# Output projection of a retention/S5/cross-attention block: model columns instead of tokens on the partitions

## Chip, cores and metric

The kernel runs on one core of a Trainium2 chip. The metric is the device time of one execution in microseconds (us); each kernel is run several times and the median is compared.

## What is computed

The reference is one block of a sequence model over 1024 tokens of 1024 features: retention and an S5 branch with an output projection and a residual, then cross-attention to a memory of 256 rows, and a final norm. The part that matters here is its end:

```python
    o = jnp.einsum('bhlm,bmhd->blhd', p, va).reshape(B, L, XA_HEADS * XA_DH)
    x = x + o @ xa_wo[l]
return rms_norm(x, norm_f_g)     # y = x * rsqrt(mean(x*x, -1) + EPS);  y * g
```

## The kernel before, in words

All activations are held transposed (features on the 128 partitions, tokens in the free dimension), each as a pair of float32r tiles, a high part and a low part. A matrix product is three matmuls per 128-deep slice of the contraction: high by high, high by low and low by high (`mm3`, lines 94 to 97). Weights come in groups of 256 columns: `get_w` (line 84) hands out the group that is ready and starts the load of the next one, which `load_w` (line 65) brings in two DMAs on the SyncE queue (line 70) and splits into its high part on ScalarE (line 74) and its low part on VectorE or GpSimd (line 75). The planner of the framework writes the order of each engine's instructions ahead of the run; the program's order is only its starting point, so work of neighbouring stages is interleaved.

The last stages (lines 902 to 1002) handle two halves of 512 tokens. `scores` and `attend` make the attention output `oT` of a half, feature-major. `wo_half` (line 944) then multiplies it by the output weights, for four groups `gi` of 256 model columns. The second half's `attend` calls are put between the groups of the first half (`between`, line 955); `wo_half` of the second half has nothing between.

In one group, `wo_half` goes over the four 128-token blocks in pairs. For each pair:

- the residual `x1`, which lies feature-major, is read from DRAM in two DMAs per group (line 953), turned by four TensorE transposes into the PSUM tile `pxps` (line 962), and copied to the tile `on` by ScalarE (line 963);
- per token block 24 matmuls (8 slices by 3) go into the PSUM tile `wops`, with 128 tokens as the stationary operand and the 256 weight columns moving (line 968);
- VectorE adds the residual (line 972), ScalarE squares with an accumulated row sum (line 974), and for the first three groups VectorE multiplies by the norm's gain (line 976).

At the fourth group `finish` (line 983) adds up the row sums (one column per token block), takes a reciprocal square root by bit trick and three Newton steps (`rsqrt`, lines 111 to 120: eleven small VectorE instructions), scales one half of the row on ScalarE (line 989) and the other on VectorE (lines 991 and 992), and sends the two pieces of 128 rows by 512 columns to the output (lines 990 and 993, SyncE queue). The PSUM pool for `wops` has two buffers of two banks.

Two helpers are used elsewhere in the program and matter here: `mean_sq` (line 271) sums squares over the partitions by matmuls against a column of ones, one matmul of one moving column per 128 tokens, and `bcast_rows` (line 122) spreads a per-token scalar over all partitions by a matmul of the scalar (broadcast to 128x128) with the identity.

Of the kernel before, what the change touches and what calls it, by code (L numbers as in the profile page):

```python
# [12 lines left out]
F32 = mybir.dt.float32  # L13
F32R = mybir.dt.float32r
I32 = mybir.dt.int32
AF = mybir.ActivationFunctionType
ALU = mybir.AluOpType
AX = mybir.AxisListType
PSUM = bass.MemoryType.PSUM

P = 128
L = 1024
D = 1024
# [7 lines left out]
EPS = 1e-6  # L31
# [14 lines left out]
def block_kernel(ctx: ExitStack, tc: tile.TileContext, a: dict):  # L46
    nc = tc.nc
    v, s, g = nc.vector, nc.scalar, nc.gpsimd
# [6 lines left out]
    small = ctx.enter_context(tc.tile_pool(name="small", bufs=2, reuse_waits="tile"))  # L55
# [6 lines left out]
    def sm_ps(shape, name="smps"):  # L62
        return psm.tile(shape, F32, tag="sm", name=name)
# [30 lines left out]
    def mm3(out, wh, wl, xh, xl, first, last):  # L94
        nc.tensor.matmul(out, wh, xh, start=first, stop=False)  # L95
        nc.tensor.matmul(out, wh, xl, start=False, stop=False)  # L96
        nc.tensor.matmul(out, wl, xh, start=False, stop=last)  # L97
# [13 lines left out]
    def rsqrt(dst, x, m, name):  # L111

        it = small.tile([P, m], I32, tag="rsq_i", name=f"i_{name}")
        t = small.tile([P, m], F32, tag="rsq_t", name=f"t_{name}")
        v.tensor_scalar(it, x.bitcast(I32), 1, None, op0=ALU.logical_shift_right)
        v.tensor_scalar(dst.bitcast(I32), it, -1.0, RSQ, op0=ALU.mult, op1=ALU.add)
        for _ in range(3):
            v.tensor_tensor(t, dst, dst, ALU.mult)
            v.scalar_tensor_tensor(t, t, -0.5, x, op0=ALU.mult, op1=ALU.mult)
            v.scalar_tensor_tensor(dst, t, 1.5, dst, op0=ALU.add, op1=ALU.mult)  # L120
# [14 lines left out]
    off = {}  # L135
# [3 lines left out]
        o += width  # L139
    ident, cmask, gv, geps, g128, gn_g = (off[z] for z in ("ident", "cmask", "gv", "geps", "g128", "gn_g"))  # L140
    g2, gm, glu_b, invf, rsgn, nsgn, psgn = (off[z] for z in ("g2", "gm", "glu_b", "invf", "rsgn", "nsgn", "psgn"))
    d4, i16 = off["d4"], off["i16"]
    g1 = gp1
    ones = const.tile([P, 1], F32, name="ones")
    v.memset(ones, 1.0)
# [53 lines left out]
    for k in range(KT):  # L199
# [5 lines left out]
        hi, lo = act_pair(k, "h")  # L205
        s.activation(w_hi[:, k, :], wr, AF.Copy)
        for c in ((slice(0, 512), slice(512, L)) if k == 0 else (slice(0, L),)):
# [3 lines left out]
                                   op0=ALU.mult, op1=ALU.subtract)  # L211
# [472 lines left out]
    for gi in range(4):  # L684
        w = get_w("w_u", gi)
        for c in range(2):
            ct = 2 * gi + c
            ps = proj_t(w, c, hT, name="ups")
            ut = ev.tile([P, 8, 8, 16], F32, tag="ut", name=f"ut{ct}", bufs=3)
            pv = ps.rearrange("p q (n j c) -> p (q n) j c", n=4, j=8)  # L690
            rb = rstd_b.rearrange("p (n j c) -> p n j c", n=8, j=8)
# [158 lines left out]
    kalo = ap_.tile([P, 8, M], F32R, name="kalo")  # L850
    vahi = ap_.tile([P, 2, D], F32R, name="vahi")
    valo = ap_.tile([P, 2, D], F32R, name="valo")
    gf = ap_.tile([P, D], F32, name="gf")
    nc.sync.dma_start(out=gf, in_=a["gf"].to_broadcast([P, D]))
    qap = ctx.enter_context(tc.tile_pool(name="qap", bufs=2, reuse_waits="tile"))

    def queries(half, h):
# [84 lines left out]
            lst.append((hi, lo))  # L942

    def wo_half(half, oT, between):
        on = [qap.tile([P, D], F32, tag=("qhi", "qlo")[t % 2], name=f"on{half}{t}") for t in range(4)]
        ssq = [small.tile([P, 5], F32, tag=f"ssq{t}", name=f"ssq{half}{t}") for t in range(4)]
        pre = [z[:, 4:5] for z in ssq]
        for gi in range(4):
            hi, lo = get_w("w_xo", gi)
            xts = []  # L950
            for c in range(2):
                xt = pp.tile([P, 512], F32, tag="xt", name=f"xt{half}{gi}{c}", bufs=4)
                nc.sync.dma_start(out=xt, in_=a["x1_d"][2 * gi + c][:, half * 512:half * 512 + 512])
                xts.append(xt)
            between(gi)
            cs = slice(gi * 256, gi * 256 + 256)
            for t0 in range(0, 4, 2):
                px = sm_ps([P, 2, 256], "pxps")
                for t in range(2):
                    ts = slice((t0 + t) * P, (t0 + t + 1) * P)  # L960
                    for c in range(2):
                        nc.tensor.transpose(px[:, t, c * P:c * P + P], xts[c][:, ts], ident)
                    s.activation(on[t0 + t][:, cs], px[:, t, :], AF.Copy)
                ps = big_ps([P, 2, 512], "wops")
                for t in range(2):
                    ts = slice((t0 + t) * P, (t0 + t + 1) * P)
                    for k in range(8):
                        mm3(ps[:, t, 0:256], oT[k][0][:, ts], oT[k][1][:, ts], hi[:, k, :], lo[:, k, :],
                            k == 0, k == 7)
                for t in range(2):  # L970
                    x2 = on[t0 + t]
                    v.tensor_tensor(x2[:, cs], ps[:, t, 0:256], x2[:, cs], ALU.add)
                    jk = pp.tile([P, 256], F32, tag="jk", name="jk", bufs=2)
                    s.activation(jk, x2[:, cs], AF.Square, accum_out=ssq[t0 + t][:, gi:gi + 1])
                    if gi < 3:
                        v.tensor_tensor(x2[:, cs], x2[:, cs], gf[:, cs], ALU.mult)
                    if gi == 2:
                        v.tensor_reduce(pre[t0 + t], ssq[t0 + t][:, 0:3], axis=AX.X, op=ALU.add)
                        v.tensor_scalar(pre[t0 + t], pre[t0 + t], 1.0 / D, EPS, op0=ALU.mult, op1=ALU.add)
                    if gi == 3:  # L980
                        finish(half, t0 + t, x2, ssq[t0 + t][:, 3:4], pre[t0 + t])

    def finish(half, t, x2, last, pre):
        ss = small.tile([P, 1], F32, tag="ssf", name="ssf")
        rf = small.tile([P, 1], F32, tag="rf", name="rf")
        v.scalar_tensor_tensor(ss, last, 1.0 / D, pre, op0=ALU.mult, op1=ALU.add)
        rsqrt(rf, ss, 1, "f")
        row = (half * 4 + t) * P
        s.activation(x2[:, 0:512], x2[:, 0:512], AF.Copy, scale=rf)
        nc.sync.dma_start(out=a["out"][row:row + P, 0:512], in_=x2[:, 0:512])  # L990
        v.scalar_tensor_tensor(x2[:, 768:D], x2[:, 768:D], rf, gf[:, 768:D], op0=ALU.mult, op1=ALU.mult)
        v.tensor_scalar(x2[:, 512:768], x2[:, 512:768], rf, None, op0=ALU.mult)
        nc.sync.dma_start(out=a["out"][row:row + P, 512:D], in_=x2[:, 512:D])

    pr0, pr1, oT0, oT1 = [], [], [], []
    for h in range(4):
# [1 line left out]
    for h in range(4):  # L998
# [13 lines left out]


CPACK = (("ident", 128), ("cmask", 128), ("gv", 8), ("geps", 8), ("g128", 4), ("gn_g", 8), ("g2", 8), ("gm", 8),
         ("glu_b", 8), ("invf", 1), ("rsgn", 1), ("nsgn", 1), ("psgn", 1), ("d4", 16), ("i16", 16))
CPW = sum(z for _, z in CPACK)


def tok_perm():
    return np.arange(L).reshape(NCH, 16, 8).transpose(0, 2, 1).reshape(L)  # L1020


def host_arrays(x, mem, positions, norm1_g, w_in, ret_gn_g, s5_a_re, s5_a_im, s5_log_dt,
# [4 lines left out]
    def c(z):  # L1028
        return np.ascontiguousarray(z)

    def col(vec):
        return c(np.asarray(vec).reshape(8, P).T)
# [14 lines left out]
    out = {}  # L1047
# [2 lines left out]
    out["g1"], out["g2"] = col(np.asarray(norm1_g)[0]), col(np.asarray(norm2_g)[0])  # L1050
    out["gm"] = col(np.asarray(norm_mem_g)[0])
    out["gn_g"] = col(np.asarray(ret_gn_g)[0])
    out["gf"] = c(np.asarray(norm_f_g).reshape(1, D))
    out["glu_b"] = col(np.asarray(s5_glu_b)[0][chp])
    out["w_kq"], out["w_v"], out["w_g"] = wg(w_kq), wg(wv), wg(wgr)
    out["w_u"], out["w_gs"] = wg(wu[:, chp]), wg(wgs[:, chp])
# [60 lines left out]
```

## Time and profile before

| | us |
|---|---|
| median of 3 runs | 1185.98 (1185.93 to 1187.71) |
| the profiled execution's own time | 1183.76 |
| span of its profile | 1182.0 |
| TensorE busy in the span | 1132.4 (96%) |
| VectorE / ScalarE / GpSimd busy | 640.4 / 451.0 / 284.6 |
| mean granted TensorE clock | 0.979 |

The span runs from the first to the last instruction of the profiled execution; 1.76 us of its own time lie outside. Below, PE is TensorE, PEld its weight load, DVE VectorE, ACT ScalarE, POOL GpSimd, SPq the SyncE queue that issues DMAs. In a row of a timeline the first number is the start in us from the beginning of the span, the second the duration in us; "x2" means that neighbouring instructions were merged. Ends of matmuls are modelled, so the steps from start to start tell more than the durations.

### The profile page before, as it was taken

What the parts mean: (1) busy time and instruction counts of PE and PEld (TensorE: products, weight loads), DVE (VectorE), ACT (ScalarE), POOL (GpSimd) and SP (SyncE); (2) the same over time, 40 slices, a digit from 0 to 9 for tenths busy, and PEclk for the clock granted to TensorE, in tenths of its full rate; (3) what the DMA queues carried; (4) which work ended last, traced back from release to release, by engine and by line L of the source; (5) the groups of instructions that cost most, each with busy time, mean ns of one, the idle gap of its engine ahead of it and who ended that gap; (6) DMA issues with size and microseconds to landing.
All of it is one profiled execution on the core that took longest, in us unless ns stands there. A gap on an engine that the chain in (4) does not pass through costs nothing.

```text
span 1182.0 us, 18361 instructions
## 1 busy us (share of the span) xinstructions
PE 1132.4 (96%) x7020; PEld 991.8 (84%) x7020; DVE 640.4 (54%) x1348; ACT 451.0 (38%) x903; POOL 284.6 (24%) x422
## 2 busy tenths in 40 slices
PE   8899689999999689999999999999999999999996
PEld 6897688898888568888888888888889888889996
DVE  7794464573662425585577216534635445554564
ACT  7322432342432312354453115224334444444453
POOL 2348798372084101212221100000320000000000
PEclk9899899999999889999999999999999999999998
DMA  6412343343241177799785349534446522222251
GB/s 233 120 52 89 98 159 131 101 153 97 55 165 58 36 225 202 212 279 276 222 268 202 133 148 279 179 124 148 137 143 197 173 77 72 72 72 72 90 197 72
DMA packets 92376, 171.88 MB, mean 145 GB/s; under 512 B 10880, under 2 KB 46976, under 8 KB 92288
## 3 DMA queue, kind: packets, MB, share of 16 engines
q1 hardware_dynamic: 92000, 170.57, 45.7%
q8 instruction: 55, 0.90, 0.3%
q14 instruction: 33, 0.27, 0.1%
q10 hardware_dynamic: 288, 0.14, 0.0%
HBM read 122.04 MB, written 44.43 MB: 141 GB/s over the span
## 4 chain that ended last, share of the span: by engine, by line
PE 59%; DMA 2%; DVE 2%; ACT 1%; issue 0%; DVEq 0%; ACTq 0%
PE wops L95 3%; PE wops L96 3%; PE wops L97 3%; PE qaps L97 3%; PE qaps L96 3%; PE gsps L97 2%; PE glups L95 2%; PE glups L97 2%; PE qaps L95 2%; PE gsps L96 2%; PE gsps L95 2%; PE obps L96 2%; PE obps L95 2%; PE obps L97 2%; PE glups L96 2%; PE oaps L97 2%
## 5 line engine op out<-in xcount | busy, mean ns | idle before, releaser
L95 PE MATMUL vps<-whi_w_v,hh 128*128 128x256 f32 x256 | 73.5, 287 | 0.7 <-ACT qs_k L290 0.7
L96 PE MATMUL vps<-wlo_w_v,hh 128*128 128x256 f32 x256 | 73.5, 287 | 0.6 <-POOL wlo_w_v L75 0.6
L95 PE MATMUL wops<-whi_w_xo,o 128*128 128x256 f32 x256 | 73.6, 288 | 0.0
L97 PE MATMUL vps<-whi_w_v,hl 128*128 128x256 f32 x256 | 73.5, 287 | 0.0
L97 PE MATMUL wops<-whi_w_xo,o 128*128 128x256 f32 x256 | 72.1, 281 | 0.0
L95 PE MATMUL gps<-whi_w_g,hh 128*128 128x256 f32 x256 | 71.9, 281 | 0.0
L96 PE MATMUL wops<-wlo_w_xo,o 128*128 128x256 f32 x256 | 71.8, 281 | 0.0
L97 PE MATMUL gps<-whi_w_g,hl 128*128 128x256 f32 x256 | 71.8, 281 | 0.0
L96 PE MATMUL gps<-wlo_w_g,hh 128*128 128x256 f32 x256 | 71.5, 279 | 0.0
L844 POOL TENSOR_TENSOR sq<-sq,sqx 128x1024 f32<-128x1024 f32 x7 | 19.0, 2717 | 196.9 <-ACT sqx L843 196.9
L95 PE MATMUL ups<-hh,whi_w_u 128*128 128x512 f32 x128 | 51.9, 406 | 1.9 <-DVE ut L692 1.9
L95 PEld LDWEIGHTS vps<-whi_w_v,hh 128*128 128x128 f32 x256 | 49.8, 194 | 1.8 <-ACT qs_k L290 1.1
L96 PE MATMUL ups<-hl,whi_w_u 128*128 128x512 f32 x128 | 51.2, 400 | 0.0
L97 PE MATMUL ups<-hh,wlo_w_u 128*128 128x512 f32 x128 | 51.2, 400 | 0.0
L96 PEld LDWEIGHTS vps<-wlo_w_v,hh 128*128 128x128 f32 x256 | 49.8, 195 | 1.6 <-POOL wlo_w_v L75 0.8
L95 PE MATMUL oaps<-reth,whi_w_oa 128*128 128x512 f32 x128 | 51.0, 398 | 0.0
L97 PE MATMUL qaps<-h,wlo_w_xq 128*128 128x512 f32 x128 | 50.6, 396 | 0.0
L95 PE MATMUL gsps<-hh,whi_w_gs 128*128 128x512 f32 x128 | 50.6, 395 | 0.0
L97 PE MATMUL gsps<-hh,wlo_w_gs 128*128 128x512 f32 x128 | 50.6, 395 | 0.0
L95 PE MATMUL qaps<-h,whi_w_xq 128*128 128x512 f32 x128 | 50.5, 394 | 0.0
L96 PE MATMUL qaps<-h,whi_w_xq 128*128 128x512 f32 x128 | 50.4, 394 | 0.0
L97 PE MATMUL oaps<-reth,wlo_w_oa 128*128 128x512 f32 x128 | 50.3, 393 | 0.0
(394 smaller groups left out, 3496.2 us busy)
## 6 DMA issues: line engine op xcount, KB each, us to landing
CS<-tab_d SPq DMA_DIRECT2D x32, 256.0 KB, 5.2
yr<-y_d SPq DMA_DIRECT2D x16, 512.0 KB, 6.2
wraw_w_xq<-w_xq SPq DMA_DIRECT2D x16, 512.0 KB, 4.1
wraw_w_xo<-w_xo SPq DMA_DIRECT2D x16, 512.0 KB, 4.4
vv_d<-VV SPq DMA_DIRECT2D x16, 288.0 KB, 2.8
VV<-vv_d SPq DMA_DIRECT2D x16, 288.0 KB, 4.3
wraw_w_v<-w_v SPq DMA_DIRECT2D x8, 512.0 KB, 4.6
wraw_w_g<-w_g SPq DMA_DIRECT2D x8, 512.0 KB, 4.8
```

Of the source, the lines that this page charges most:

```text
L95: nc.tensor.matmul(out, wh, xh, start=first, stop=False)
L96: nc.tensor.matmul(out, wh, xl, start=False, stop=False)
L97: nc.tensor.matmul(out, wl, xh, start=False, stop=last)
L844: g.tensor_tensor(sq2, sq2, sq, ALU.add)
```

## The change

The projection is turned over: the weight columns become the stationary operand (128 model columns) and 512 tokens move, so the result comes out feature-major, as the residual lies in DRAM. The transposes of the residual and their ScalarE copies are gone; VectorE adds the residual straight from the loaded tile. Squares are summed in a tile `acc` over the eight column blocks (the additions on GpSimd, in the last group on VectorE), and `finish` then sums `acc` over the partitions by `mean_sq`, takes the reciprocal square root for up to four token blocks in one chain, spreads it over the partitions by matmuls into PSUM (`rb`), and scales eight column blocks on VectorE, each with its gain as a per-partition scalar, each followed by its own output DMA. In the last group of the second half the 512 tokens are handled in two parts of 256. The output tensor is laid out (8, 128, 1024) and is turned back on the host. The gain comes in the packed constants instead of a 512 KB broadcast load.

```diff
-    gf = ap_.tile([P, D], F32, name="gf")
-    nc.sync.dma_start(out=gf, in_=a["gf"].to_broadcast([P, D]))
...
     def wo_half(half, oT, between):
-        on = [qap.tile([P, D], F32, tag=("qhi", "qlo")[t % 2], name=f"on{half}{t}") for t in range(4)]
-        ssq = [small.tile([P, 5], F32, tag=f"ssq{t}", name=f"ssq{half}{t}") for t in range(4)]
-        pre = [z[:, 4:5] for z in ssq]
+        x2 = [qap.tile([P, 2, 512], F32, tag=("qhi", "qlo")[t % 2], name=f"x2_{half}{t}") for t in range(4)]
+        acc = pp.tile([P, 512], F32, tag="acc", name=f"acc{half}", bufs=2)
         for gi in range(4):
...
             between(gi)
...
+            parts = [slice(0, 512)] if gi < 3 or half == 0 else [slice(0, 256), slice(256, 512)]
+            for ts in parts:
                 ps = big_ps([P, 2, 512], "wops")
+                for c in range(2):
+                    cs = slice(c * P, c * P + P)
                     for k in range(8):
-                        mm3(ps[:, t, 0:256], oT[k][0][:, ts], oT[k][1][:, ts], hi[:, k, :], lo[:, k, :],
-                            k == 0, k == 7)
...
+                        mm3(ps[:, c, ts], hi[:, k, cs], lo[:, k, cs], oT[k][0][:, ts], oT[k][1][:, ts], k == 0, k == 7)
+                    xo = x2[gi][:, c, ts]
+                    v.tensor_tensor(xo, ps[:, c, ts], xts[c][:, ts], ALU.add)
+                    if gi == 0 and c == 0:
+                        s.activation(acc, xo, AF.Square)
+                    else:
+                        sq = pp.tile([P, 512], F32, tag="sqo", name=f"sqo{half}{gi}{c}", bufs=2)
+                        s.activation(sq[:, ts], xo, AF.Square)
+                        (v if gi == 3 else g).tensor_tensor(acc[:, ts], acc[:, ts], sq[:, ts], ALU.add)
+                if gi == 3:
+                    finish(half, ts, x2, acc)
...
+    def finish(half, ts, x2, acc):
+        n = (ts.stop - ts.start) // P
+        msf = small.tile([P, 4], F32, tag="msf", name="msf")
+        rf = small.tile([P, 4], F32, tag="rf", name="rf")
+        mean_sq(msf[:, :n], acc[:, ts], n, "f")
+        rsqrt(rf[:, :n], msf[:, :n], n, "f")
+        rb = sm_ps([P, 512], "rbps")
+        for j in range(n):
+            nc.tensor.matmul(rb[:, j * P:j * P + P], bc(rf[:, j:j + 1], [P, P]), ident, start=True, stop=True)
+        for ct in range(8):
+            xo = x2[ct // 2][:, ct % 2, ts]
+            v.scalar_tensor_tensor(xo, xo, gfc[:, ct:ct + 1], rb[:, 0:n * P], op0=ALU.mult, op1=ALU.mult)
+            nc.sync.dma_start(out=a["out"][ct][:, half * 512 + ts.start:half * 512 + ts.stop], in_=xo)
```

## Rows read from the trace of the kernel before

**Rows 1.** The page's first part: busy time, share of the span, instructions.

```profile
PE 1132.4 (96%) x7020; PEld 991.8 (84%) x7020; DVE 640.4 (54%) x1348; ACT 451.0 (38%) x903; POOL 284.6 (24%) x422
```

**Rows 2.** Busy us (count) of PE, PEld, DVE, ACT, POOL; PEclk, DMA share, GB/s.

```profile
1058.70:1172.80 114.10, 114.10 (x937) 111.61 (x935) 63.93 (x207) 53.34 (x149) 0.00 (x0) 1.00 0.31 105
1172.80:1182.00 9.20, 0.03 (x1) 0.00 (x0) 4.64 (x30) 2.36 (x6) 0.00 (x0) 0.65 0.52 195
```

**Rows 3.** The chain that ended last, two pieces of it, around the last matmuls.

```profile
1169.87 0.22 PE pxps L962 x2
...
1172.87 0.44 DVE on L972
```

**Rows 4.** Groups by line and shape, 1058 to 1182 us; busy us, mean ns.

```profile
L972 DVE TENSOR_TENSOR on<-wops,on 128x256 f32<-128x256 f32 x32 | 12.7, 421 | 39.3 <-PE wops L97 21.6 <-ACT o L940 9.1 <-ACT on L963 8.5
L976 DVE TENSOR_TENSOR on<-on,gf 128x256 f32<-128x256 f32 x24 | 9.8, 422 | 3.9 <-ACT jk L974 3.8
```

**Rows 5.** Timeline of PE, output projection: a quick run of matmuls and a slow one.

```profile
1164.02 0.28 PE L96 MATMUL wops<-wlo_w_xo,o 128*128 128x256 f32 x1
...
1166.54 0.28 PE L97 MATMUL wops<-whi_w_xo,o 128*128 128x256 f32 x1
...
1167.11 0.28 PE L97 MATMUL wops<-whi_w_xo,o 128*128 128x256 f32 x1
...
1169.58 0.28 PE L97 MATMUL wops<-whi_w_xo,o 128*128 128x256 f32 x1
```

**Rows 6.** Timeline of PE in the gating stage: first and last of 18 matmuls of 512 columns.

```profile
775.01 0.39 PE L95 MATMUL glups<-yh,whi_w_glu 128*128 128x512 f32 x1
...
778.90 0.39 PE L97 MATMUL glups<-yh,wlo_w_glu 128*128 128x512 f32 x1
```

**Rows 7.** Timeline of PE around the memory's norm (two token blocks).

```profile
838.09 0.50 PE L274 MATMUL ms_m<-ones,sqm 128*128 128x1 f32 x4
838.45 0.49 PE L96 MATMUL obps<-ssmlo,whi_w_ob 128*128 128x512 f32 x1
...
845.84 0.60 PE L128 MATMUL bcps<-cp,rm 128*128 128x128 f32 x4
846.21 0.48 PE L95 MATMUL obps<-ssmhi,whi_w_ob 128*128 128x512 f32 x1
```

**Rows 8.** Timeline of DVE there: scaling of 512 columns, first and last of the norm.

```profile
833.95 1.42 DVE L837 SCALAR_TENSOR_TENSOR h<-x,cp,h 128x512 fp32r<-128x512 f32 x2 [0.79 <-ACT h L836]
838.62 0.16 DVE L275 TENSOR_SCALAR msm<-ms_m 128x2 f32<-128x2 f32 x1 [3.25 <-PE ms_m L274]
...
840.79 0.16 DVE L120 SCALAR_TENSOR_TENSOR rm<-t_m,rm 128x2 f32<-128x2 f32 x1
```

**Rows 9.** Timeline of ACT and DVE after the last matmul.

```profile
1173.39 0.42 ACT L974 ACTIVATE jk<-on 128x256 f32<-128x256 f32 x1 [1.47 <-DVE on L972]
...
1173.93 0.16 DVE L986 SCALAR_TENSOR_TENSOR ssf<-ssq 128x1 f32<-128x1 f32 x1 [0.30 <-ACT jk L974]
...
1176.26 0.16 DVE L119 SCALAR_TENSOR_TENSOR t_f<-t_f,ssf 128x1 f32<-128x1 f32 x1
...
1176.33 0.48 DVE L991 SCALAR_TENSOR_TENSOR on<-on,rf,gf 128x256 f32<-128x256 f32 x1
1176.73 0.35 DVE L992 TENSOR_SCALAR on<-on,rf 128x256 f32<-128x256 f32 x1
1176.99 0.16 DVE L120 SCALAR_TENSOR_TENSOR rf<-t_f,rf 128x1 f32<-128x1 f32 x1
```

**Rows 10.** Timeline of the SyncE queue: first and last of the four closing DMA issues.

```profile
1177.08 0.33 SPq L990 DMA_DIRECT2D out<-on  x1
...
1178.48 0.40 SPq L993 DMA_DIRECT2D out<-on  x1
```

**Rows 11.** The view by stretches, while the closing DMAs moved (columns as in rows 2).

```profile
1177.00:1181.50 4.50, 0.00 (x0) 0.00 (x0) 0.90 (x4) 0.78 (x2) 0.00 (x0) 0.50 0.63 233
```

**Rows 12.** Page, costliest groups: additions of squares on GpSimd.

```profile
L844 POOL TENSOR_TENSOR sq<-sq,sqx 128x1024 f32<-128x1024 f32 x7 | 19.0, 2717 | 196.9 <-ACT sqx L843 196.9
```

More of the change, by code (lines that the diff above doesn't have):

```diff
@@ L141, in block_kernel @@
     g2, gm, glu_b, invf, rsgn, nsgn, psgn = (off[z] for z in ("g2", "gm", "glu_b", "invf", "rsgn", "nsgn", "psgn"))
-    d4, i16 = off["d4"], off["i16"]
+    d4, i16, gfc = off["d4"], off["i16"], off["gf"]
     g1 = gp1
@@ L955, in wo_half @@
             between(gi)
[L956 to L963, printed above, removed]
+            parts = [slice(0, 512)] if gi < 3 or half == 0 else [slice(0, 256), slice(256, 512)]
@@ L964, in wo_half @@
+            for ts in parts:
                 ps = big_ps([P, 2, 512], "wops")
-                for t in range(2):
-                    ts = slice((t0 + t) * P, (t0 + t + 1) * P)
+                for c in range(2):
+                    cs = slice(c * P, c * P + P)
                     for k in range(8):
-                        mm3(ps[:, t, 0:256], oT[k][0][:, ts], oT[k][1][:, ts], hi[:, k, :], lo[:, k, :],
-                            k == 0, k == 7)
[L970 to L993, printed above, removed]
+                        mm3(ps[:, c, ts], hi[:, k, cs], lo[:, k, cs], oT[k][0][:, ts], oT[k][1][:, ts], k == 0, k == 7)
@@ L1014 @@
 CPACK = (("ident", 128), ("cmask", 128), ("gv", 8), ("geps", 8), ("g128", 4), ("gn_g", 8), ("g2", 8), ("gm", 8),
-         ("glu_b", 8), ("invf", 1), ("rsgn", 1), ("nsgn", 1), ("psgn", 1), ("d4", 16), ("i16", 16))
+         ("glu_b", 8), ("invf", 1), ("rsgn", 1), ("nsgn", 1), ("psgn", 1), ("d4", 16), ("i16", 16), ("gf", 8))
 CPW = sum(z for _, z in CPACK)
@@ L1052, in host_arrays @@
     out["gn_g"] = col(np.asarray(ret_gn_g)[0])
-    out["gf"] = c(np.asarray(norm_f_g).reshape(1, D))
+    out["gf"] = col(norm_f_g)
     out["glu_b"] = col(np.asarray(s5_glu_b)[0][chp])
@@ L1107 @@
            for n, z in arrays.items()}
-    aps["out"] = nc.dram_tensor("out", (L, D), F32, kind="ExternalOutput").ap()
+    aps["out"] = nc.dram_tensor("out", (8, P, L), F32, kind="ExternalOutput").ap()
     with tile.TileContext(nc, schedule_with_timeline_sim=True) as tc:
@@ L1114 @@
     out = np.empty((L, D), np.float32)
-    out[tok_perm()] = np.asarray(r.results[0]["out"])
+    out[tok_perm()] = np.asarray(r.results[0]["out"]).reshape(D, L).T
     return out.reshape(1, L, D)
```

## The prediction, made before the changed kernel ran

> **What bounds the kernel now.** The page's first part comes first: PE is busy for 96% of the span, no other engine above 54% [rows 1]. Next the view by stretches. From the first output projection to its end PE is busy for 114.1 of 114.1 us at full clock, while DVE and ACT are busy for 64 and 53 of them [rows 2]. So in that stretch only what PE executes counts, and relief for DVE, ACT or the queues is worth nothing. Behind it stand 9.2 us in which PE does nothing: a chain of small steps and the last DMAs. Third, the chain of waits shows what PE's pieces cost there, and where DVE takes over, at 1172.87 [rows 3]; I call that moment E. From E to the end of the span are 1182.0 - 1172.87 = 9.13 us. The change works on both stretches, with opposite signs. Sums are made against the profiled execution (1183.76 us, 2.2 under the median of the runs shown) and then put onto the median, 1185.98. A difference of less than 0.2%, 2.4 us, counts as no change.
>
> **PE's stretch, part by part.**
>
> The transposes go: 2 halves x 4 groups x 8 = 64, two of which take 0.22 us of the chain [rows 3]: -7.0 us. Their ACT copies, the gain products and ACT's row sums go too, at 0, since PE covers them.
>
> Wide steps: 672 matmuls of 256 columns become 336 of 512; 96 stay narrow (the last group of the second half). A narrow step is 2.52/22 = 0.1145 us in a quick run and 2.47/21 = 0.1176 in a slow one [rows 5], two of them 0.2290 to 0.2352. A wide one is 3.89/17 = 0.2288 [rows 6]. So 336 x (0.0002 to 0.0064) = 0.1 to 2.2 us are saved; neither run is the nearer, so the middle: -1.1. Halving the weight loads gives no more than that: the wide row already has one load per step.
>
> New on PE: sums over partitions and spreading. For two token blocks the four instructions of the sum take 0.36 us and push the next step to 0.32 instead of 0.23, in all 0.45; the spreading takes 0.37 and the same push, 0.45 again [rows 7]. The first half has four blocks: 0.9 + 0.9 = +1.8. The first part of the last group has two: +0.9. The second part's lie behind E.
>
> VectorE and others inside the stretch, at 0: in the first half DVE scales eight tiles of 512 columns at 0.71 us each [rows 8], 5.7 us, beside the next group's 48 wide steps (11 us). If that cover goes, the next low weights or the first addition of the second half, which also waits for the first tile's output DMA, come up to 5.7 us late; the two PSUM buffers let PE run a further 11 us ahead of the additions. GpSimd has five additions per half at about half of 2.7 us (estimate from [rows 12]) against 11 us per group. The first half issues eight output DMAs of 256 KB, as before; they wait on the SyncE queue for DVE, and the weight loads behind them are wanted a group later. The gain's 512 KB load early in the attention stage goes, off the path.
>
> **The tail.** The second part's own chain, every step after E: the addition starts, its square 0.52 later, DVE again at 1.06 [rows 9]; adding to `acc` 0.42, as an addition of that shape takes [rows 4], 1.48; sum over partitions, from its start to the scalar on DVE, 0.53 [rows 7, 8], 2.0; scalar and square root 2.33 (838.62 to 840.95) [rows 8], 4.35; spreading 0.60 [rows 7], 4.95. Scaling starts at E + 5.0 at the earliest. Its first tile takes 0.48 [rows 9]; then the eight DMA issues stand on one queue, 1.40/3 = 0.47 us apart [rows 10], which is slower than DVE's 0.40 per tile [rows 9]: the last issue starts at 5.0 + 0.5 + 7 x 0.47 = E + 8.8. From the last issue to the end of the span it is 3.5 us now [rows 10]. That gives E + 12.3, or +3.2 against 9.13: lower bound of the tail's growth.
>
> In its way stands the first part's scaling. That part's last matmul lies 48 x 0.116 + 0.9 = 6.5 us ahead of E, its chain takes the same 5.0, so its eight tiles begin about E - 1.5 and need 8 x 0.40 = 3.2: 1.7 us of them lie behind E. DVE takes work that stands earlier in the program first: the scaling of one token block went ahead of the last two steps of the other's square root, and L120 followed L119 by 0.73 us instead of 0.2 [rows 9]. So I put 1.7 us in front of the second part's chain: +4.9. If the first part's sum or spreading is held in PE's queue, as the memory's spreading ran 4.9 us after its scalar was ready (840.95 to 845.84) [rows 7, 8], all 3.2 us can come behind E: +6.4, upper bound. I take +4.9, the value worked out from the rows of the order, half way between the two. The last sum and spreading run after PE has been idle, where the granted clock falls to its half level (0.50 in [rows 11]); up to 0.4 more at the upper end.
>
> [...] DVE's additions with one input in PSUM and with both in SBUF take 421 and 422 ns for 256 columns [rows 4], so scaling against a spread scalar in PSUM is charged like scaling from SBUF, at 0 extra. [...]
>
> **Sum:** -7.0 - 1.1 + 1.8 + 0.9 + 4.9 = -0.5 us. Bounds: -7.0 - 2.2 + 2.7 + 3.2 = -3.3 and -7.0 - 0.1 + 2.7 + 6.4 + 0.4 = +2.4. On the median: 1185.5, from 1182.7 to 1188.4. What PE saves, the tail gives back.
>
> **Rivals.**
>
> *The tail stays short (faster).* DVE lets the second part's chain through and does the rest of the first part's scaling in the gaps while ACT squares, PE sums and PE spreads; those gaps sum to 0.1 + 0.5 + 0.6, against 1.7 us wanted. Then the tail grows by 3.2 and the sum is -2.2, with quick wide steps -3.3: about 1183.2. For it: the work fits nearly. Against: the order seen in [rows 9].
>
> *PE waits for a norm (slower).* PE takes its instructions in order. If the first half's sum over partitions is queued straight behind that half's last product, PE stands through addition, square and addition (1.5 us, and about 0.9 more at 512 columns, by the 0.71 against 0.42 of rows above), and if the spreading follows straight on, through the 2.33 us square root too: 4.7 us, so +4.2, 1190.2. It decides where fewer than 2.4 us, ten wide steps, are queued in front of the sum or of the spreading. Against: at the memory's norm, the same pair of steps, PE ran other products for 7.3 us between sum and spreading and never stood [rows 7].
>
> *The output drains slowly (slower).* Rows of the last pieces are 1 KB long, half of before. 1 MB in four pieces moved at 233 GB/s at the end [rows 11], 4.5 us; the second part's 1 MB leaves within 3.7 us of issues. If short rows cut the rate to 150 GB/s, it takes 7 us and the end moves by 3: +2.5, 1188.5. It decides below about 230 GB/s. [...] Against: four pieces left 0.47 us apart and moved side by side.
>
> *The change doesn't do what it says:* wide steps that save nothing lie inside the bounds (-1.1 becomes -0.1).
>
> **How the numbers follow.** Forecast 0.58, of which 0.04 end above +2.4. Short tail 0.22, of which 0.02 end within 2.4 us. PE waits 0.10. Slow drain 0.08. Something unlisted that is faster 0.02. So faster 0.22, no change 0.54 + 0.02 = 0.56, slower 0.04 + 0.10 + 0.08 = 0.22. The range reaches from the lower bound, 1182.7, which is also the fast rival's, over the slow drain to 1189.2, a part of the PE rival: left out are about one case in ten above and as many below.
>
> **What would show it.** Right: PE fully busy through the projection and its last product about 5.4 us earlier on the span; wide steps near 0.229 us; the end 13.5 to 15 us after the last product; tiles of the first part being scaled after E and ahead of the second part's square root; output issues about 0.47 us apart. Wrong: idle PE between the halves, with the first half's sum or spreading behind it; the second part's square root ahead of the first part's scaling; issues that wait for DMAs; a stretch that shrinks by clearly more or less than 5 us. The forecast falls as a whole if the planner moves work elsewhere in the program.

## The result, and the profile after

The changed kernel takes 1207.9 us (median of 5 runs, 1204.7 to 1210.2), the kernel before beside it 1185.9: a ratio of 1.0182, 95% interval 1.0169 to 1.0195. It is slower by 22 us, far outside the predicted range. The profiled execution took 1204.69 us with a span of 1202.9, 20.9 more than before. The first page rows of the changed kernel, which answer to [rows 1]:

```profile
span 1202.9 us, 17475 instructions
...
PE 1145.5 (95%) x6652; PEld 980.0 (81%) x6652; DVE 633.6 (53%) x1248; ACT 429.8 (36%) x817; POOL 299.1 (25%) x432
```

PE executes 368 instructions fewer and is busy 13 us longer. So the loss isn't only one of waiting: PE's work itself took longer.

Cut at the first product of the output projection and at the start of the last addition, as in the prediction, the span divides into three pieces (us, read from the timelines of PE and DVE):

| | first product | last addition | end | projection | tail |
|---|---|---|---|---|---|
| before | 1058.70 | 1172.87 | 1182.0 | 114.17 | 9.13 |
| after | 1066.21 | 1187.83 | 1202.9 | 121.62 | 15.07 |

So +7.51 before the projection begins, +7.45 in it, +5.94 behind it. Each piece has a view of its own.

**Before the projection.** The order of PE's instructions up to the first output product is the same in both kernels, and no line of the diff changes one of them. But the steps are longer. The timeline of PE in the gating stage of the changed kernel, two matmuls 18 steps apart, answers to [rows 6]:

```profile
780.14 0.39 PE L97 MATMUL glups<-yh,wlo_w_glu 128*128 128x512 f32 x1
...
784.34 0.39 PE L97 MATMUL glups<-yh,wlo_w_glu 128*128 128x512 f32 x1
```

4.20/18 = 0.2333 us a step, against 3.89/17 = 0.2288 before. The granted clock is 1.00 there in both kernels (775.0 to 779.2 before, 780.0 to 784.5 after). From the first product of `ups`, the recurrence's input projection (367.06 before, 368.58 after), to the first output product this adds up to 6.0 us.

**In the projection.** The view by stretches (columns as in [rows 2]) has the whole projection, two slices of it between the halves, and the tail:

```profile
1066.21:1187.83 121.62, 112.87 (x559) 94.42 (x558) 53.67 (x109) 34.47 (x68) 14.68 (x10) 0.94 0.29 96
1140.00:1150.00 10.00, 2.61 (x14) 2.26 (x13) 6.79 (x20) 0.00 (x0) 0.00 (x0) 0.59 0.33 124
1150.00:1160.00 10.00, 8.82 (x29) 7.03 (x30) 2.68 (x5) 1.82 (x4) 0.00 (x0) 0.72 0.45 140
1187.83:1202.90 15.07, 2.17 (x12) 1.66 (x10) 9.15 (x30) 0.42 (x1) 0.00 (x0) 0.67 0.42 139
```

PE was busy for 114.1 of 114.1 us before; now it stands for 8.75, most of them between 1140 and 1150, and the granted clock falls with it, to 0.59 there. The timeline of PE there:

```profile
1139.62 0.95 PE L274 MATMUL ms_f<-ones,acc 128*128 128x1 f32 x8
1143.08 2.05 PE L979 MATMUL rbps<-cp,rf 128*128 128x128 f32 x8 [2.52 <-DVE rf L120]
1151.18 0.80 PE L95 MATMUL wops<-o,whi_w_xo 128*128 128x512 f32 x1 [6.05 <-DVE x L961]
1151.77 0.63 PE L96 MATMUL wops<-o,whi_w_xo 128*128 128x512 f32 x1
1152.20 0.63 PE L97 MATMUL wops<-o,wlo_w_xo 128*128 128x512 f32 x1
```

Sum over partitions, spreading and the next product follow each other with nothing between. Ahead of the sum PE had already run the first column block of the second half's first two groups, 48 products that need no addition, the last of them at 1139.38. The product at 1151.18 opens the second column block of the first of these groups, in the same PSUM tile, and waits for the first block's addition. So PE waits 2.52 us for the root and 6.05 us for that addition, and the next steps are 0.43 us long, at a granted clock of 0.50, until 1155.4. The timeline of DVE shows what the addition stood behind:

```profile
1145.17 5.36 DVE L982 SCALAR_TENSOR_TENSOR x<-x,cp,rbps 128x512 f32<-128x512 f32 x8 [2.23 <-PE rbps L979]
1150.44 1.28 DVE L961 TENSOR_TENSOR x<-wops,xt 128x512 f32<-128x512 f32 x2
```

The first half's eight scalings come first, and only then the second half's first additions.

**The tail.** The timeline of DVE from the last addition on answers to [rows 9] (the rows of the root are left out):

```profile
1187.83 0.42 DVE L961 TENSOR_TENSOR x<-wops,xt 128x256 f32<-128x256 f32 x1 [0.56 <-PE wops L97]
1188.27 3.22 DVE L982 SCALAR_TENSOR_TENSOR x<-x,cp,rbps 128x256 f32<-128x256 f32 x8
1191.41 0.42 DVE L967 TENSOR_TENSOR acc<-acc,sqo 128x256 f32<-128x256 f32 x1
1192.59 0.16 DVE L275 TENSOR_SCALAR msf<-ms_f 128x2 f32<-128x2 f32 x1 [0.76 <-PE ms_f L274]
...
1196.29 3.22 DVE L982 SCALAR_TENSOR_TENSOR x<-x,cp,rbps 128x256 f32<-128x256 f32 x8 [1.38 <-PE rbps L979]
```

The timeline of the SyncE queue, where [rows 10] had four issues:

```profile
1188.78 11.78 SPq L983 DMA_DIRECT2D out<-x  x16
```

All eight scalings of the first part lie behind the last addition and in front of the second part's sum; its own scalings begin at E + 8.5, where the prediction's sum has E + 6.7 (5.0 and the 1.7 in front). The sixteen output issues follow DVE, and the span ends 2.3 us after the last of them has been issued.

### The profile page after: what moved, and what is told of

Its sections match the earlier page's. It is cut to its first block, busy times and chain, and to the rows that moved or that the text cites. A ratio compares the mean times of both kernels' runs of the same rounds, so it can differ in the third digit from the quotient of the medians.

```text
span 1202.9 us, 17475 instructions
## 1 busy us (share of the span) xinstructions
PE 1145.5 (95%) x6652; PEld 980.0 (81%) x6652; DVE 633.6 (53%) x1248; ACT 429.8 (36%) x817; POOL 299.1 (25%) x432
## 4 chain that ended last, share of the span: by engine, by line
PE 79%; POOL 8%; DVE 5%; DMA 4%; issue 2%; ACT 1%; SPq 0%; DVEq 0%; POOLq 0%; ACTq 0%
PE wops L95 3%; PE wops L97 3%; PE wops L96 3%; PE glups L96 2%; PE qaps L95 2%; PE qaps L97 2%; PE glups L95 2%; PE glups L97 2%; PE qaps L96 2%; PE ups L95 2%; PE ups L96 2%; PE obps L96 2%; PE obps L97 2%; PE obps L95 2%; PE ups L97 2%; PE gsps L95 2%
## 5 line engine op out<-in xcount | busy, mean ns | idle before, releaser
L967 POOL TENSOR_TENSOR acc<-acc,sqo 128x512 f32<-128x512 f32 x10 | 14.7, 1468 | 265.1 <-issue 190.1
L95 PE MATMUL wops<-o,whi_w_xo 128*128 128x512 f32 (+1 forms) x144 | 54.3, 377 | 6.2 <-DVE x L961 6.2
L97 PE MATMUL wops<-o,wlo_w_xo 128*128 128x512 f32 (+1 forms) x144 | 54.1, 376 | 0.0
L96 PE MATMUL wops<-o,whi_w_xo 128*128 128x512 f32 (+1 forms) x144 | 53.9, 374 | 0.0
L96 PE MATMUL gsps<-hl,whi_w_gs 128*128 128x512 f32 x128 | 50.7, 396 | 0.0
```

Of the source, the lines that this page charges most:

```text
L967: (v if gi == 3 else g).tensor_tensor(acc[:, ts], acc[:, ts], sq[:, ts], ALU.add)
```

## The experiments

The first theory after this reading had three parts. (1) *Placement*: the gain put eight columns more into the packed constants, 32 bytes per partition, everything allocated behind them moved by 32 bytes, and PE's steps grew with that. (2) *The addition inside the loop*: the first column block's addition stands between the two blocks' products, so that PE can't finish a group without DVE. (3) *The tail* as predicted.

### Placement alone: e1_pad8, e2_own

e1 is the kernel before with eight columns that nobody reads; e2 is the changed kernel with its gain in a tile of its own and the constants as they were.

```diff
 e1 (before):  -  ... ("i16", 16))
               +  ... ("i16", 16), ("pad", 8))
 e2 (after):   -  ... ("i16", 16), ("gf", 8))
               +  ... ("i16", 16))
+    gf = ap_.tile([P, D], F32, name="gf")
+    gfc = gf[:, 0:8]
+    nc.sync.dma_start(out=gfc, in_=a["gf"])
```

> The kernel before, with eight unused columns added to the packed constants, so that everything allocated behind them in SBUF lies 32 bytes higher. Theory (placement): the steps of the 512-column matmuls from the recurrence's input projection to the queries go from about 229-230 ns to 233 ns, as in the changed kernel, and the time grows by 6 to 10 us, to about 1194 us. Rival (the slow steps come with the changed program or with the run): steps stay at 229-230 ns and the time at 1186 us, within 2 us.

> The changed kernel, with the gain in a tile of its own in place of the old broadcast tile, so that the packed constants and all behind them lie as before. Theory (placement): the first product of the output projection starts near 1059 us instead of 1066 us, steps are 229-230 ns again, and the time falls from 1207.9 by 7 to 10 us to 1198-1201 us; the wait between the halves stays. Rival: steps of 233 ns and 1207 us.

Measured: e1 1195.3 us, ratio to the kernel before 1.0082 (1.0053 to 1.0111); e2 1197.8, 1.0098 (1.0083 to 1.0113), 0.2 us under the expected range. Eight unused columns cost the kernel before 0.8%, and taking them out of the changed kernel gives 0.8% back. The timeline of PE in e2's gating stage, again 18 steps:

```profile
776.50 0.39 PE L97 MATMUL glups<-yh,wlo_w_glu 128*128 128x512 f32 x1
...
780.62 0.39 PE L97 MATMUL glups<-yh,wlo_w_glu 128*128 128x512 f32 x1
```

4.12/18 = 0.2289: the step of before. About 10 of the 22 us are the place of the tiles. In the profiled executions e2's span is 7.1 us shorter than the changed kernel's: 4.6 of that lie ahead of the projection and 2.4 in it, where the wide steps shorten as well.

### Products ahead of the additions: e3_evac, e4_own_evac

```diff
                 for c in range(2):
                     cs = slice(c * P, c * P + P)
                     for k in range(8):
                         mm3(ps[:, c, ts], ...)
+                for c in range(2):
                     xo = x2[gi][:, c, ts]
                     v.tensor_tensor(xo, ps[:, c, ts], xts[c][:, ts], ALU.add)
```

e4 has the gain's own tile too.

> The changed kernel, with both column blocks of a group multiplied before the first is added to the residual, so that no product waits for the addition of the other block in the same PSUM tile. Theory (product waits for the addition, which stands behind the first half's scaling on DVE): PE's idle stretch between the halves, about 8.5 us with 3 us of half clock behind it, goes; the time falls by 9 to 12 us to 1196-1199 us; the slow steps and the tail stay. Rival (PE stands there because the norm's sum and spreading are queued back to back): idle time of 2.5 us and more stays in front of the spreading, and the time falls by 6 us at most.

> Both of the last two together: the change without its shift of placement and without the wait of one block's products for the other's addition. If the two are independent causes: 1207.9 - 8.5 - 10.5 = about 1189 us, of which the tail after the last product is 15 us against 9.1 us in the kernel before; between 1186 and 1191 us. If there is a further cause, it stays above 1192 us.

Measured: e3 1202.7, ratio 1.0138 (1.0122 to 1.0155), 5.1 us off the changed kernel where 9 to 12 were expected. That is the time of its rival, but not the rival's mechanism: in e3 the first half's sum (1139.95) and spreading (1150.41) lie 10.5 us of products apart, and PE doesn't wait for that root. e4 takes 1194.5, 1.0069 (1.0052 to 1.0085), above the bound that was to mean a further cause. The waits of PE in e4's projection and tail:

```profile
PE rbps L983 <- DVE rf L120: 7.8, 2, 5.3
PE wops L95 <- ACT acc L967: 4.6, 1, 4.6
```

The first row is the tail's. The second lies between the halves, at 1142.6, when PE had run all products of the second half's first two groups and both PSUM buffers were full. The row names ACT's square, the last to end before PE went on (1147.52); but that square reads `x2` and no PSUM. In the compiled program PE's next product waits for the two additions that empty the first group's buffer, and these end at 1147.45, 0.15 us before PE goes on. DVE there, in e4's timeline:

```profile
1140.30 5.36 DVE L986 SCALAR_TENSOR_TENSOR x<-x,gf,rbps 128x512 f32<-128x512 f32 x8 [5.79 <-PE rbps L983]
1145.57 0.68 DVE L75 TENSOR_TENSOR wlo_w_xo<-wraw_w_xo,whi_w_xo 128x512 fp32r<-128x512 f32 x1
1146.17 1.28 DVE L965 TENSOR_TENSOR x<-wops,xt 128x512 f32<-128x512 f32 x2
```

DVE stood idle for 5.79 us ahead of the scalings, and the second half's first group was there by then (its last product started at 1130.73). It couldn't add the residual to that group: `x2` of both halves has the tags `qhi` and `qlo` with two buffers each, so the second half's four tiles *are* the first half's four tiles. The additions overwrite what the scalings have still to read and the output DMAs have still to send. With the tiles shared, the loop's place was worth some 3 us (e2 to e4) to 5 us (changed kernel to e3); the shared tiles are the theory that follows.

### Other tiles for the second half: e5_tiles, e12_own_tiles

```diff
-        x2 = [qap.tile([P, 2, 512], F32, tag=("qhi", "qlo")[t % 2], name=f"x2_{half}{t}") for t in range(4)]
+        if half == 0:
+            x2 = [qap.tile([P, 2, 512], F32, tag=("qhi", "qlo")[t % 2], name=f"x2_{half}{t}") for t in range(4)]
+        else:
+            x2 = [pp.tile([P, 2, 512], F32, tag="prob", name=f"x2_{half}{t}", bufs=5) for t in range(4)]
```

The probabilities' tiles are free by then and have the size. e5 is e4 with this edit, e12 is e2 with it (additions back in the loop).

> Own gain tile, both blocks' products ahead of the additions (as in e4_own_evac, 1194.5 us), and the second half's four residual sums in tiles of their own instead of the first half's. Theory: in e4 the second half's first additions start at 1146.17 because they overwrite tiles that the first half's eight scalings (1140.30 to 1145.66) and their output transfers must have read, and the weight splits of DVE stand behind the same scalings; TensorE idles about 4.6 us there and runs at half clock after it. With other tiles the additions come ahead of the scalings: that wait goes, and the run takes 1188 to 1191 us (4 to 6 us off e4). Rival (TensorE idles because the products run ahead of the weight splits whatever the additions do): within 1.5 us of e4, above 1192.5. The tail stays at 16 to 17 us from the start of the last group's first addition of its second part.

> Own gain tile and tiles of its own for the second half's sums, but the additions where the change has them, inside the loop over the two column blocks (e5_tiles without e3's edit). Theory: the first block's addition then stands between the two blocks' products, the planner mixes one group's first block with the next one's, and the products wait for DVE between the halves; 1188 to 1193 us, with a wait of wops for a DVE addition. Rival: with the tiles free, the place of the additions costs nothing, 1184 to 1186 us, as e5_tiles.

Measured: e5 1185.0 us, ratio 0.9991 (0.9973 to 1.0009), 9.5 off e4 where 4 to 6 were expected; e12 1186.7, 0.9998 (0.9982 to 1.0013), where the rival had 1184 to 1186 and the theory of the loop 1188 to 1193; between the halves of e12 no product waits for DVE. So the pair e2 and e12 puts the shared tiles at 0.0100 of 1186, some 12 us. With the tiles free, the loop's place costs nothing that can be told (e5 and e12 lie within each other's intervals). e5 by stretches, columns as in [rows 2]:

```profile
1130.00:1140.00 10.00, 10.00 (x47) 8.27 (x47) 6.49 (x18) 3.24 (x6) 1.30 (x1) 1.00 0.46 150
1140.00:1150.00 10.00, 10.00 (x49) 8.39 (x48) 8.02 (x13) 3.42 (x6) 1.19 (x1) 1.00 0.66 245
```

And the timeline of its DVE between the halves:

```profile
1131.70 1.29 DVE L968 TENSOR_TENSOR x<-wops,xt 128x512 f32<-128x512 f32 x2
...
1141.98 5.36 DVE L989 SCALAR_TENSOR_TENSOR x<-x,gf,rbps 128x512 f32<-128x512 f32 x8 [4.68 <-PE rbps L986]
1147.25 1.28 DVE L968 TENSOR_TENSOR x<-wops,xt 128x512 f32<-128x512 f32 x2
```

The second half's first additions come 10 us ahead of the scalings, and PE is busy throughout at full clock (1.00). The sum over partitions and the spreading lie 11.4 us of products apart (1129.46 and 1140.89), as they did in e4 (10.3); e12, with the additions in the loop, has 11.2 where e2 has 3.5. The scalings, which I had charged at 0, do cost 0 here, with 5.36 us as they were.

### The tail: e6_once, e7_nosplit

e6 spreads both parts' roots into one tile and scales once, 512 wide, behind both; e7 drops the split of the last group. Both are built on e4.

```diff
 e6:  -    def finish(half, ts, x2, acc):            (sum, root, spreading, scaling per part)
      +    def norm(half, ts, x2, acc, rb):          (sum, root, spreading per part)
      +        scale((half, slice(0, 512), x2, rb, 4))     behind both parts
 e7:  -            parts = [slice(0, 512)] if gi < 3 or half == 0 else [slice(0, 256), slice(256, 512)]
      +            parts = [slice(0, 512)]
```

> As e4_own_evac (1194.5 us), but the last group's two token parts share one tile of spread norms and the eight output blocks are scaled once, 512 wide, behind both parts' roots, with 8 output transfers instead of 16. Theory of the tail: in e4 the first part's eight scalings (3.22 us) stand in DVE's queue ahead of the second part's root; without them the root ends about 3 us earlier, and the scalings then take 5.36 instead of 3.22 us: a gain of 1 to 2 us, 1192.5 to 1193.5 us. Rival (the tail is set by the sixteen output transfers on SP's queue, 10.6 us of issues): a gain of 3 us or more. Third: splitting the scaling is what pays, and one scaling is slower by 1 us or more.

> As e4_own_evac (1194.5 us), but the last group is not split into two token parts: additions, squares, sums, root, spreading and scaling once, 512 wide. By e4's durations the way behind the last product is 2 additions (1.28 us), a square and a sum (0.63 + 0.68), ones matmuls and their latency (0.7), root (2.3), spreading (1.2 at half clock with its latency 0.4 more), eight scalings (5.36) and the last output (about 2.5): 15 us from the last product, against 1189.7 - 1172.5 = 17.2 us in e4. If so, 1192 to 1194 us, and the split buys nothing. If the split hides what it was meant to hide, 1196 us or more.

Measured: e6 1192.8 (ratio 1.0059, 1.0038 to 1.0080), e7 1192.6 (1.0068, 1.0046 to 1.0091), against 1194.5 for e4. Both lie in the ranges that the theory of DVE's queue gave: the first part's scalings stand ahead of the second part's root, and splitting the group buys nothing. The gains of 1.7 and 1.9 us themselves are not shown: against the kernel before, measured beside each, the ratios differ from e4's by 0.0010 and 0.0001, within intervals of 0.2% each. e6's tail in DVE's timeline:

```profile
1177.09 0.16 DVE L275 TENSOR_SCALAR msf<-ms_f 128x2 f32<-128x2 f32 x1 [1.76 <-PE ms_f L274]
...
1180.74 5.36 DVE L991 SCALAR_TENSOR_TENSOR x<-x,gf,rbps 128x512 f32<-128x512 f32 x8 [1.32 <-PE rbps L985]
```

The second part's root begins 4.1 us after the last addition (1172.95) instead of 6.3 in e4; the wider scalings take most of that back.

### What the place of a tile does: e8_pad16, e9_right, e10_place, e11_best

e8 is the kernel before with 16 unused columns instead of e1's eight. e9 leaves the left of SBUF alone and puts the activations 64 bytes lower. e10 lets the weights of the 512-column stages begin 64 bytes later in longer tiles, e11 does the same to e5, `w_xo` included.

```diff
 e8:  +  ("pad", 16)
 e9:  +    act.tile([P, 16], F32, tag="shift", name="shift")
 e10: +    def w_tile(tag, name):
      +        t = wpool.tile([P, KT * 256 + 64], F32R, tag=tag, name=f"{tag}_{name}")
      +        o = 16 if name.startswith(("w_kq", "w_u", "w_gs", "w_oa", "w_glu", "w_xq")) else 0
      +        return t[:, o:o + KT * 256].rearrange("p (k c) -> p k c", k=KT)
```

> The kernel before with 16 unused columns in the packed constants (64 bytes a partition instead of the 32 of e1_pad8, which took 1195.3 us with 233 ns a step). If the step depends on whether the streams lie at a multiple of 64 bytes, this one is as fast as before: 229 to 230 ns and 1184 to 1188 us. If any shift is a loss, or the step has other values at other places (227 ns is seen in one stage of every kernel), 1176 to 1182 us or 1190 to 1197 us.

> The kernel before, with the activations' tiles (the other side of SBUF, moving operand of the 512-column products) 64 bytes lower and the weights left where they are. By the program's addresses, modulo 256 bytes, weights and activations lie at 160 and 224 in the kernel before (steps of 229.5 ns at 512 columns, 114 at 256), at 192 and 224 in e1_pad8 (233, 118), at 224 and 224 in e8_pad16 (227, 120); here at 160 and 160. If the step depends on how stationary and moving operand lie to each other, this run has e8's steps: 227 to 228 ns at 512 columns and 119 to 120 at 256, and takes 1184 to 1192 us. If it depends on the place of the weights alone, it has the steps of before, 229 to 230 and 114 to 117.

> The kernel before, with the split weights of the 512-column stages (w_kq, w_u, w_gs, w_oa, w_glu, w_xq) 64 bytes further in tiles that are 256 bytes longer, so at 224 like the activations; the weights that move themselves, 256 columns at a time (w_v, w_g, w_xk, w_xv, w_xo), stay at 160, and all other tiles keep their place modulo 256. If the place of the two operands to each other sets the step: 227 to 228 ns in the 512-column stages and 114 to 117 in the 256-column ones, over 1920 wide steps and more at 2.4 ns each, so 4 to 7 us less than before: 1179 to 1183 us. If not: as before, within 1.5 us.

> e5_tiles (1185.0 us) with the same placing, here with w_xo too at 224, since in the changed kernel it stands still and the activations move: 227 to 228 ns a step from the retention's end to the output projection, 384 wide steps more than in e10, so 5 to 8 us less than e5_tiles: 1177 to 1180.5 us, below both kernels.

Two rows of the timeline of PE carry each step. For e8, first the gating stage (weights stand still, 512 activation columns move), 18 steps apart:

```profile
781.21 0.39 PE L97 MATMUL glups<-yh,wlo_w_glu 128*128 128x512 f32 x1
...
785.29 0.39 PE L97 MATMUL glups<-yh,wlo_w_glu 128*128 128x512 f32 x1
```

Then the retention's gate (activations stand still, 256 weight columns move), 20 steps apart:

```profile
178.07 0.28 PE L97 MATMUL gps<-whi_w_g,hl 128*128 128x256 f32 x1
...
180.47 0.28 PE L96 MATMUL gps<-wlo_w_g,hh 128*128 128x256 f32 x1
```

4.08/18 = 0.2267 and 2.40/20 = 0.1200. The kernel before has 0.2288 for the first, and for the gate these rows of its timeline, 2.27/20 = 0.1135:

```profile
176.87 0.28 PE L95 MATMUL gps<-whi_w_g,hh 128*128 128x256 f32 x1
...
179.14 0.28 PE L97 MATMUL gps<-whi_w_g,hl 128*128 128x256 f32 x1
```

The same reading for all kernels, over 65 to 67 steps of the gating stage and 76 to 100 of the gate, beside the places of the operands, which are the addresses of the compiled programs modulo 256 bytes (weights in the gating stage / activations):

| kernel | weights / activations | 512 columns, ns | 256 columns, ns | median us | ratio |
|---|---|---|---|---|---|
| before | 160 / 224 | 228.9 | 113.6 | 1185.9 | 1 |
| after | 192 / 224 | 233.2 | 118.3 | 1207.9 | 1.0182 |
| e1_pad8 | 192 / 224 | 233.4 | 118.4 | 1195.3 | 1.0082 |
| e8_pad16 | 224 / 224 | 226.7 | 119.9 | 1187.6 | 1.0015 (0.9996 to 1.0035) |
| e9_right | 160 / 160 | 226.7 | 119.9 | 1187.3 | 1.0011 (0.9999 to 1.0024) |
| e10_place | 224 / 224, moving weights 160 | 226.7 | 113.5 | 1179.7 | 0.9953 (0.9936 to 0.9969) |
| e11_best | 224 / 224, moving weights 160 | 226.7 | 113.5 | 1182.0 | 0.9975 (0.9956 to 0.9994) |

e8's time is the one its expectation gave for unchanged steps, but the steps are not unchanged. e9 moved the other operand and has e8's steps to the tenth of a ns. So it isn't the weights' own place that counts but how the two operands lie to each other: equal places give the shortest wide step and the longest narrow one, 64 bytes apart a middling wide step and the shortest narrow one, and 32 apart, as the change had it, the longest wide step and a long narrow one. That fits the one stage of the kernel before that ran at 227 ns, `obps`, whose moving tiles lie at 160 like the weights.

The place isn't all of it. With the operands 64 bytes apart, the same instructions run at two levels within one execution. In the stage of the queries in the kernel before, 18 steps each, at a granted clock of 1.00 (935 to 940 and 968 to 973), with other matmuls between the two stretches:

```profile
935.40 0.39 PE L97 MATMUL qaps<-h,wlo_w_xq 128*128 128x512 f32 x1
...
939.52 0.39 PE L97 MATMUL qaps<-h,wlo_w_xq 128*128 128x512 f32 x1
...
968.68 0.40 PE L95 MATMUL qaps<-h,whi_w_xq 128*128 128x512 f32 x1
...
972.88 0.40 PE L95 MATMUL qaps<-h,whi_w_xq 128*128 128x512 f32 x1
```

That is 0.2289 and 0.2333. The quick and the slow run of narrow steps in [rows 5] are such a pair too. So the table's figures are those of the two stretches read, not of every step of a kernel, and what picks the level is not shown.

e8 gains in one kind of step what it loses in the other, and its time is that of before. e10 takes the better of each and comes out 0.47% faster than the kernel before, as expected. e11 missed: 3 us below e5 instead of 5 to 8, though its wide steps are as expected; from the first product of `ups` to the first output product it needs 687.9 us against 692.8 in e5, so the steps did pay, but it begins `ups` at 367.7, 2.5 us later than e5. About 1.6 of these 2.5 us are the two levels: the retention's gate steps average 114.7 ns in e11 against 113.5 in e5, and those of its values 116.4 against 115.3, some 700 steps each. Ahead of that point other kernels with the same place of the narrow steps differ too (366.6 in e10, 367.3 in e2).

Both e10 and e11 beat the kernel before and the changed one; the lowest median is that of the old projection with better placed weights (e10), though the intervals of the two overlap.

## Why the prediction was wrong

Some of the profiled executions on one scale (us, read as in the first table; the last two columns are differences). Each row is a single execution, and the first column differs by up to 4 us among the five kernels other than the changed one, whose steps ahead of the projection have the same places:

| | first product | last addition | end | projection | tail |
|---|---|---|---|---|---|
| before | 1058.70 | 1172.87 | 1182.0 | 114.2 | 9.1 |
| after | 1066.21 | 1187.83 | 1202.9 | 121.6 | 15.1 |
| e2_own | 1061.63 | 1180.84 | 1195.8 | 119.2 | 15.0 |
| e4_own_evac | 1057.50 | 1173.20 | 1189.7 | 115.7 | 16.5 |
| e12_own_tiles | 1059.31 | 1166.77 | 1184.5 | 107.5 | 17.7 |
| e5_tiles | 1058.05 | 1166.33 | 1183.2 | 108.3 | 16.9 |

**PE's own work: right.** The steps -7.0 - 1.1 + 1.8 + 0.9 gave -5.4 for the projection. Where nothing else disturbs it, it shrinks by 5.9 (e5) and 6.7 (e12). The whole sum, -0.5 us, is within what e5 and e12 show: ratios of 0.9991 and 0.9998, no difference that can be told. That agreement is partly luck, since the tail is 2.8 and 3.7 us longer there than forecast.

**"The two PSUM buffers let PE run a further 11 us ahead of the additions": the step that failed.** The prediction saw that the second half's first addition waits for the first half's output, and that it could come late; it charged 0 because of that cover. In the changed kernel the cover had been used up: no product stands between the sum over partitions at 1139.62 and the end of the wait at 1151.18. The 48 products that the two buffers allow without an addition, the prediction's 11 us, had been planned ahead of the sum, and the next one waits for an addition that stands behind the scalings. So the root's 2.3 us, the spreading's 2.05 and the scalings' 5.4 lay open on PE, and the half clock after the idle time (0.50 from 1151.18 to 1155.4) came on top. Measured by e2 and e12: 12 us on the median, where the prediction has 0. The cover needed other tiles for the second half's additions to write into, and that was the one thing the change didn't give it.

**The packed constants: a step that wasn't there.** The prediction counted the 512 KB load that goes, "off the path", and gave the eight columns that come no price at all. They cost 10 us, by moving tiles, mostly of stages that the diff doesn't touch. The shared tiles alone put the time above the predicted range (e2, 1197.8 us); these 10 us alone, on e12's 1186.7, would have done so too. No row of the trace of before gives that price; what one could have seen is that equal matmuls take different steps there, narrow ones 0.1145 and 0.1176 in [rows 5], wide ones 227 ns in `obps` and 229 or 233 in the queries, so that the step depends on something besides its size.

**The tail: mechanism right, 1 us short.** Predicted +4.9, between +3.2 and +6.4; measured +5.9 in the changed kernel. The first part's scalings do stand ahead of the second part's chain, but with all 3.2 us behind E instead of 1.7. The 1 us is a difference of two errors: the last issue starts 1.8 us later than the sum has it (E + 12.3 instead of 10.5), and from there to the end it takes 2.7 us instead of 3.5. In e5 and e12 the tail is 7.7 and 8.6 longer than before, outside the bounds: there PE's queue adds to it, since the second part's sum stands behind the first part's spreading. The timeline of PE in e12:

```profile
1169.86 1.22 PE L985 MATMUL rbps<-cp,rf 128*128 128x128 f32 x4 [2.78 <-DVE rf L120]
1170.87 0.85 PE L274 MATMUL ms_f<-ones,acc 128*128 128x1 f32 x4
```

The squares were summed by 1168.2, and the sum over partitions ran at 1170.87.

**The rivals.** *PE waits for a norm* was the nearest: sum and spreading did follow straight on, with 2.52 us of waiting between them. But its price counts only waits for the norm; the wait behind it, 6.05 us for an addition, was not in it. *The tail stays short* is out. *The output drains slowly* is out as well: the span ends 2.3 us after the last output issue. *Wide steps that save nothing* came true in the changed kernel (233 ns against two narrow ones of 116 before), but not because of their shape: with the operands where e2 has them they take 229.

**Scaling from PSUM: right.** Eight scalings of 256 columns against a spread scalar in PSUM take 3.22 us, 0.40 each, as charged, and no more than the 0.42 of [rows 4].

## What to carry to other kernels

When a normalisation moves behind a whole half of the tokens, ask which tiles its inputs stay in and who wants to write them next: a shared tag turned 5.4 us of "covered" VectorE work into 12 us on the critical engine, and four other tiles removed them. When a diff changes the size of anything that is allocated early, compare the steps of stages that it doesn't touch before reading anything else; this kernel, bound by TensorE, lost 0.8% by 32 bytes (e1) and won 0.5% by 64 in the right place (e10). And a change whose gain is given back in the tail, as here, is worth less than it looks even when all goes well: the kernel before with some of its weights moved by 64 bytes has the lowest median of this study.

## What the runs showed of the hardware that was not expected

In the stretches of the table, a matmul step of 512 float32r columns took 226.7, 228.9 or 233.3 ns, and one of 256 columns 113.5, 118.4 or 119.9 ns, in the same program order and at a granted clock of 1.00 (160 to 195 and 775 to 790, in the kernel before and the changed one), by the place of its stationary and moving operands to each other, read modulo 256 bytes (0, 32 and 64 bytes apart were run, 96 and 128 were not, and whether the pattern repeats after 256 was not tried). At 64 bytes apart a second level was seen in other stretches, 233 and 118 ns. Why equal places are good for one shape and bad for the other was not settled. The two stages of the table also differ in which operand stands still. The memory's keys have 256 columns with the weights standing still, as in the wide steps, and there too equal places give the longest step, so for equal places the column count decides and not the side. For e8, 18 steps apart:

```profile
902.29 0.28 PE L95 MATMUL kaps<-mhi,whi_w_xk 128*128 128x256 f32 x1
...
904.45 0.28 PE L95 MATMUL kaps<-mhi,whi_w_xk 128*128 128x256 f32 x1
```

And for the kernel before, with the operands 64 bytes apart:

```profile
887.48 0.28 PE L95 MATMUL kaps<-mhi,whi_w_xk 128*128 128x256 f32 x1
...
889.60 0.28 PE L95 MATMUL kaps<-mhi,whi_w_xk 128*128 128x256 f32 x1
```

That is 0.1200 and 0.1178; in e1, 32 bytes apart, this stage has 0.1167. So whether 32 or 64 bytes apart is the better does change with the side. In the stretches of the table the place made a difference of 3% of a wide step (226.7 to 233.4 ns) and 5.6% of a narrow one (113.5 to 119.9).

After PE had stood 2.5 and 6.05 us with little between, the granted clock was 0.59 over 1140 to 1150, and steps of 512 columns took 0.43 us for 4 us after the work was back; the same steps took 0.23 us at a granted clock of 1.00 (1156.5 to 1158). In e5, where PE doesn't stand, that loss is absent: 1.00 in every 10 us from 1120 to 1160.
